# A two-block transformer kernel: other order of the attention heads in block 2, and its query copies issued by ScalarE

## The chip, the cores and the metric

The kernel runs on one core of a Trainium2 chip. Its time is the device time of one execution in microseconds. Engines are named as in the profile: PE is TensorE (PEld its weight loads), DVE is VectorE, ACT is ScalarE, POOL is GpSimd, SP is SyncE. A name with a q (SPq, ACTq) is the engine's sequencer, which also issues DMAs.

## The reference

Input x is 512 tokens by 1024. Block 1 (once) mixes latent attention and a state-space scan. Block 2 runs twice, layer 0 and layer 1; the change lies in its attention. Cut to what matters:

```python
def second_block(x, ...):
    for l in range(2):
        h = rms_norm(x, g_pre_mix[l])
        nq, kc, vc, ksel, vsel, kwin, vwin, gates, fq, fk, fv, ff = split(h @ w_in[l])
        o_nsa = nsa_mixer(nq, kc, vc, ksel, vsel, kwin, vwin, gates, ...)   # 8 heads of 64, 2 kv groups
        o_fox = fox_mixer(fq, fk, fv, ff, b_forget[l])                      # 8 heads of 64
        x = x + rms_norm(concat([o_nsa, o_fox]) @ w_out[l], g_post_mix[l])
        h = rms_norm(x, g_pre_mlp[l])
        x = x + rms_norm(square(relu(h @ w_up[l])) @ w_down[l], g_post_mlp[l])

# nsa, per head: a gated sum of three attentions of one query: over 31 compressed keys
#   (a small MLP over blocks of 32 tokens), over selected blocks, over a window; the last
#   two use rotary queries and keys, and with 512 tokens both see every earlier key.
# fox, per head: causal attention with logits q.k/8 + cum[i] - cum[j], cum = cumsum(log_sigmoid(f))
```

All of it is float32.

## The kernel before

**Arithmetic.** A float32 number is held as a high and a low part (ACT casts the high part, L143; DVE or POOL subtracts for the low part, L144 and L864), and one product is three matmuls (L174 to L176). A projection job is 24 such matmuls of 512 columns, and its weights (512 KB) come by one DMA on SP's queue (L153), then a high cast on ACT and a low part on DVE.

**Heads in pairs.** Queries and keys are worked on two heads at a time, 64 rows each: four nsa pairs n0 to n3 and four fox pairs f0 to f3 in each layer. An nsa pair is four runs of `attend` (two heads by two branches) and a fox pair is two. One `attend` makes scores on PE (L914 with the high, L917 with the low query), masks and takes the minimum on DVE (L918), exponentials on ACT (L921), scales on POOL (L930), transposes on PE (L943), splits (L143 and L144), and makes the values on PE (L952, L953).

**The doubled query.** A score matmul has the high and low parts of the keys stacked in its 128 rows, so the 64 rows of a query must stand there twice. `doubled` (L869) casts each head's high half (L874, L875), subtracts the low half on POOL (L864), and copies all four to the other 64 rows by DMAs of 128 KB, one `move` (L866) each: two called qh, two called ql. Eight pairs in two layers make 16 doublings and 64 moves, 32 qh and 32 ql. In the kernel before, SP issues them (L867), in one queue with all weight loads.

**What sets the order.** The program is written as generators that interleave: `rounds` runs the heads in the order of the list ORDER, and between the pieces of a head `fill` and `chunk` put pieces of the projections, in the order of the list PROJ; (0, m) is the nsa query of pair m, (1, m) the fox query, (2, m) the fox key. A scheduler with a simulated timeline then orders the instructions of each engine. Every engine and every queue works in order, so an instruction that waits holds what stands behind it. Successive projections use one PSUM bank: the next starts once ACT has copied the last out (`raw`, L1109).

**The start of a layer.** After two matmul groups for the keys (`kf`, L1083), projections run until raw (0, 0) is there, so n0's query and, by the scheduler, one more stand ahead of the compress matmuls `cps` (L983), which need weights that SP loads (L980, x9 at a time). Rotary copies of nsa queries go by small DMAs that ACT issues (`swap`, L1068). The list ORDER also sets the layout in which the pairs are summed by the output weights w_out_t, whose loads and matmuls for the finished pairs (`early`) run beside the last heads.

Of the kernel before, what the change touches and what calls it, by code (L numbers as in the profile page):

```python
# [9 lines left out]
F32 = mybir.dt.float32  # L10
# [9 lines left out]
EPS = 1e-6  # L20
NEG = -1e30
SLOTS1 = {"S": 6, "PT": 4, "E": 2, "et": 1, "K": 1, "T": 3, "Y": 1, "sq": 3, "c": 2, "PW": 1, "U": 1, "C": 1, "w": 4}
PROJ = ((0, 0), (2, 0), (1, 0), (0, 1), (2, 1), (1, 1), (0, 2), (2, 2), (1, 2), (0, 3), (2, 3), (1, 3))
ORDER = "n0 f0 n1 f1 n2 f2 n3 f3".split()
PRE = 10
R0, C0, LEAD, RATE0, RATE, AHEAD = 0, 1, 1, 1.3, 0.4, 5
HEAD0 = (0, 3, 6, 9)
# [36 lines left out]
class Net:  # L64
# [799 lines left out]
        self.nc.gpsimd.tensor_tensor(out, src, hi.bitcast(F32), OP.subtract)  # L864

    def move(self, out, src):  # L866
        self.nc.sync.dma_start(out.bitcast(F32), src.bitcast(F32))  # L867

    def doubled(self, src, tag):  # L869

# [127 lines left out]
    def layer(self, l, normed, x_dram, out=None):  # L998
# [86 lines left out]
        foxt, nsat, cht, raw = {}, {}, {}, {}  # L1085

        jobs = [("k" if i == 2 else "q", i, m) for i, m in PROJ]
        loaded = []
# [6 lines left out]
        def project(j):  # L1095

            _, i, m = jobs[j]
            if j == 0:
                load()
            wh, wl = loaded[j]  # L1100
            p = self.ps("mm")
            for k in range(8):
                if k == AHEAD:
                    load()
                self.mm3(self.tiled(p), wh[k], wl[k], xh[k], xl[k], k == 0, k == 7)
                if k < 7:
                    yield
            r = raw[i, m] = self.act(name="raw", tag="S")
            nc.scalar.activation(r, p, AF.Copy, scale=-0.125 if i == 2 else 1.0)  # L1109
            if i == 0:  # L1110
                yield
                nsat[m] = self.doubled(rope(r, None), "Q")
            elif i == 1:
                foxt["q", m] = self.doubled(r, "Q")
            else:
                foxt["k", m] = self.stacked(r, "PT")

        def ensure(i, m):
            while m not in nsat if i == 0 else ("qk"[i - 1], m) not in foxt:
                self.chunk()  # L1120
            yield

        self.fillers, self.pe = [project(j) for j in range(len(jobs))], None
        while (0, 0) not in raw:
            self.chunk()
        kk = []
        for kf in kfs:
            rope(kf, kf)
            kk.append(self.stacked(kf, "K"))
        for _ in ensure(0, 0):  # L1130
            pass

        def bank(d, tag):

# [120 lines left out]
        def early():  # L1255
# [8 lines left out]
            for n in range(2 * EB):  # L1264
                while (ORDER[n][0], int(ORDER[n][1])) not in whole:
                    yield
                self.mm3(p, *(x[:, 0:128] for x in mixed[ORDER[n][0], int(ORDER[n][1])]), wo[0][n], wo[1][n], n == 0, False)
                part.append(n)
# [18 lines left out]
        r = R0  # L1287
        for pair in ORDER:
            m = int(pair[1])
# [21 lines left out]
        xT, xh, xl = self.new_xT()  # L1311
        mixed = [mixed[p[0], int(p[1])] for p in ORDER]
        for half in range(2):
# [139 lines left out]
def layout(i):  # L1453
# [11 lines left out]
    w = n("w_out_2").reshape(L, 2, 4, 128, 2, 512)  # L1465
    w = np.stack([w[:, "nf".index(p[0]), int(p[1])] for p in ORDER], axis=1)
    A["w_out_t"] = w.reshape(L, 4, 2, 128, 2, 512).transpose(0, 4, 1, 3, 2, 5)
# [59 lines left out]
```

## Time and profile before

| what | us |
| --- | --- |
| time, median of 3 runs | 1667.33 (1665.48 to 1668.69) |
| the profiled execution | 1673.57 |
| its span, first to last instruction | 1671.8 |
| attention of layer 0, from its first kf to the MLP's transposes | 391.4 to 639.8 |
| attention of layer 1, the same | 1051.8 to 1313.9 |
| PE busy in the span | 1593.8 (95%) |
| ACT busy in the span | 794.3 (48%) |

The profiled execution took 6.24 us more than the median of the runs, and 1.77 us of it lie around the span. Busy shares are averages: in a stage where PE is nearly always busy, the few places where it is idle say which other engine or transfer is late there. Beside busy time, the granted clock says at which speed PE worked.

### The profile page before, as it was taken

To read this page: it belongs to the slowest core of one execution; us is meant where nothing else is said; L and a number is where in the kernel's file an instruction comes from. 1 tells how busy PE (TensorE), PEld (TensorE's weight loads), DVE (VectorE), ACT (ScalarE), POOL (GpSimd) and SP (SyncE) were. 2 spreads that over 40 slices of the span, in tenths; PEclk is the share of its full clock that TensorE was granted. 3 is DMA by queue.
4 is the path that set the end of the run, shared out by engine and by line. 5 is a ranking of instruction groups with operands and counts; after the bars stand their busy time and mean duration, and the time that the engine had idled before them with its cause. 6 is when DMAs were issued, how large, how long until landed. Compare 5 with 4: busy or idle time off the path is not lost.

```text
span 1671.8 us, 22665 instructions
## 1 busy us (share of the span) xinstructions
PE 1593.8 (95%) x8240; PEld 1345.8 (80%) x8240; DVE 951.2 (57%) x1863; ACT 794.3 (48%) x1548; POOL 402.4 (24%) x492
## 2 busy tenths in 40 slices
PE   7996899999999999999999999999989999999998
PEld 6884687787888888888888888788868888888886
DVE  8978767754687865323333365478875532333334
ACT  6634476543677845333232444368774433323242
POOL 2000013313455712001010140345580210101012
PEclk9998899999999999999999999899999999999999
DMA  5211452544322442332333334512234133333332
GB/s 172 75 56 38 129 146 76 184 119 156 92 59 53 119 134 75 96 95 89 101 101 101 114 109 128 161 45 58 64 102 126 51 101 101 101 101 101 101 96 81
DMA packets 71407, 167.44 MB, mean 100 GB/s; under 512 B 14464, under 2 KB 23168, under 8 KB 71296
## 3 DMA queue, kind: packets, MB, share of 16 engines
q1 hardware_dynamic: 70528, 165.21, 32.3%
q8 instruction: 65, 1.06, 0.3%
q10 hardware_dynamic: 768, 0.79, 0.2%
q14 instruction: 46, 0.38, 0.1%
HBM read 145.80 MB, written 10.98 MB: 94 GB/s over the span
## 4 chain that ended last, share of the span: by engine, by line
PE 70%; DVE 7%; ACT 3%; issue 3%; DMA 2%; POOL 1%; ACTq 1%; DVEq 0%; POOLq 0%; SPq 0%
PE mm L176 19%; PE mm L174 19%; PE mm L175 19%; PE cps L983 2%; PE ptr L943 2%; DVE sc L918 1%; DVE pt L144 1%; PE sc L917 1%; PE sc L914 1%; PE oacc L952 1%; PE oacc L953 1%; DVE wlo L144 1%; ACT ysq L206 1%; DMA ql<-ql 1%; ACT sc L921 1%
## 5 line engine op out<-in xcount | busy, mean ns | idle before, releaser
L144 DVE TENSOR_TENSOR wlo<-wst,whi 128x1024 fp32r<-128x1024 f32 (+3 forms) x209 | 253.7, 1218 | 248.8 <-ACT whi L143 245.1
L174 PE MATMUL mm<-xT,whi 128*128 128x512 f32 (+1 forms) x896 | 337.8, 380 | 4.3 <-ACT kf L1083 2.8
L143 ACT CAST whi<-wst 128x1024 fp32r<-128x1024 f32 (+3 forms) x209 | 215.3, 1034 | 256.6 <-PE mm L176 123.7
L175 PE MATMUL mm<-xT,whi 128*128 128x512 f32 (+1 forms) x896 | 335.5, 376 | 0.0
L176 PE MATMUL mm<-xT,wlo 128*128 128x512 f32 (+1 forms) x896 | 326.3, 376 | 0.9 <-DVE wlo L144 0.8
L1367 POOL TENSOR_TENSOR relu<-relu 128x512 f32<-128x512 f32 x64 | 67.1, 1048 | 539.6 <-ACT relu L1366 539.6
L176 PE MATMUL mm<-whi,hl 128*128 128x512 f32 x512 | 195.9, 389 | 0.0
L175 PE MATMUL mm<-wlo,hh 128*128 128x512 f32 x512 | 195.9, 389 | 0.0
L174 PEld LDWEIGHTS mm<-xT,whi 128*128 128x128 f32 x896 | 168.2, 189 | 33.4 <-ACT kf L1083 3.6
L176 PEld LDWEIGHTS mm<-xT,wlo 128*128 128x128 f32 x896 | 168.7, 189 | 32.1 <-DVE wlo L144 1.8
L175 PEld LDWEIGHTS mm<-xT,whi 128*128 128x128 f32 x896 | 168.9, 189 | 27.4
L174 PE MATMUL mm<-whi,hh 128*128 128x512 f32 x512 | 188.2, 389 | 0.0
L921 ACT ACTIVATE sc<-sc,mn 128x512 f32<-128x512 f32 x192 | 107.1, 559 | 32.9 <-DVE mn L918 25.2
L144 DVE TENSOR_TENSOR hl<-relu,hh 128x512 fp32r<-128x512 f32 x64 | 51.8, 810 | 119.4 <-ACT hh L143 117.1
L144 DVE TENSOR_TENSOR pt<-ptr,pt 128x256 fp32r<-128x256 f32 (+1 forms) x160 | 95.7, 605 | 40.0 <-ACT pt L143 39.1
L176 PEld LDWEIGHTS mm<-whi,hl 128*128 128x128 f32 x512 | 96.1, 188 | 20.0
L175 PEld LDWEIGHTS mm<-wlo,hh 128*128 128x128 f32 x512 | 96.1, 188 | 19.9
L174 PEld LDWEIGHTS mm<-whi,hh 128*128 128x128 f32 x512 | 96.1, 188 | 19.9
L1366 ACT ACTIVATE relu<-mm 128x512 f32<-128x512 f32 x64 | 38.3, 598 | 148.3 <-PE mm L176 148.3
L918 DVE CUSTOM_DVE_ANT_0 sc<-sc,c_mask 128x512 f32<-128x512 f32 x192 | 87.3, 483 | 34.2 <-PE sc L917 30.9
L143 ACT CAST pt<-ptr 128x256 fp32r<-128x256 f32 (+1 forms) x160 | 81.5, 515 | 52.4 <-PE ptr L943 41.3
L930 POOL TENSOR_SCALAR sc<-sc,smx,gt 128x512 f32<-128x512 f32 (+3 forms) x128 | 78.9, 627 | 82.9 <-DVE smx L925 54.4
(394 smaller groups left out, 2961.5 us busy)
## 6 DMA issues: line engine op xcount, KB each, us to landing
wst<-in_w_up_t SPq DMA_DIRECT2D x64, 512.0 KB
wst<-in_w_down_t SPq DMA_DIRECT2D x64, 512.0 KB
wst<-in_w_in_m SPq DMA_DIRECT2D x24, 512.0 KB
wst<-in_w_in_a SPq DMA_DIRECT2D x16, 512.0 KB
x<-x SPq DMA_DIRECT2D x32, 256.0 KB
w<-in_cw SPq DMA_DIRECT2D x32, 256.0 KB
wst<-in_w_out_t SPq DMA_DIRECT2D x16, 512.0 KB
wst<-in_w_in SPq DMA_DIRECT2D x8, 512.0 KB
```

The source lines that it names most:

```text
L143: self.nc.scalar.copy(hi, src)
L144: self.nc.vector.tensor_tensor(lo, src, hi.bitcast(F32), OP.subtract)
L174: mm(ps, lh, rh, start=first, stop=False)
L175: mm(ps, lh, rl, start=False, stop=False)
L176: mm(ps, ll, rh, start=False, stop=last)
L918: nc.vector.tensor_tensor_reduce(out=sreg[i], in0=p, in1=self.mask[:, 512 - w:512], scale=1.0, scalar=3e38, op0=OP.add, op1=OP.min, accum_ ...
L921: self.mark = nc.scalar.activation(sreg[i], sreg[i], AF.Exp, bias=mn[:, i:i + 1], scale=-1.0, accum_out=sm[:, i:i + 1])
L930: nc.gpsimd.tensor_scalar(sreg[i], sreg[i], sm[:, i:i + 1], rgate[:, i:i + 1], OP.mult, OP.mult)
L943: self.pe = nc.tensor.transpose(p[:, c:c + 128], sreg[i][:, j * 128:(j + 1) * 128], self.ident)
L983: nc.tensor.matmul(p[:, :62], st[:, j], bk[:, jj].rearrange("p g n -> p (g n)"), start=jj == 0, stop=jj == 15)
L1366: nc.scalar.activation(a, p, AF.Relu)
L1367: nc.gpsimd.tensor_tensor(a, a, a, OP.mult)
```

## The change

The order of the pairs becomes f0 n0 f1 n1 f2 n2 f3 n3 instead of n0 f0 n1 f1 n2 f2 n3 f3. The projections of pair m come as fox key, fox query, nsa query. At the start of a layer, projections run until f0's query is doubled instead of until n0's is projected, and n0's doubling is no longer finished ahead of the heads. All `move` DMAs are issued by ACT instead of SP.

```diff
-PROJ = ((0, 0), (2, 0), (1, 0), (0, 1), (2, 1), (1, 1), (0, 2), (2, 2), (1, 2), (0, 3), (2, 3), (1, 3))
-ORDER = "n0 f0 n1 f1 n2 f2 n3 f3".split()
+PROJ = tuple((i, m) for m in range(4) for i in (2, 1, 0))
+ORDER = "f0 n0 f1 n1 f2 n2 f3 n3".split()
...
     def move(self, out, src):
-        self.nc.sync.dma_start(out.bitcast(F32), src.bitcast(F32))
+        self.nc.scalar.dma_start(out.bitcast(F32), src.bitcast(F32))
...
-        while (0, 0) not in raw:
+        while ("q", 0) not in foxt:
             self.chunk()
...
-        for _ in ensure(0, 0):
-            pass
```

ACT at the start of layer 0, before. A row is line, operation, out<-in; whi is the high cast of a projection's weights, kf and raw copy PSUM out (raw_3800 is the first projection), swap the rotary DMA, ka and kb the stacked keys:

```order
L1083 ACTIVATE kf_3761<-mm_3736 128x512
L143 CAST whi_3912<-wst_3910 128x1024
L1068 DMA swap1_3285<-kf_3761 8x512 x4
L143 CAST whi_4040<-wst_4038 128x1024
L1109 ACTIVATE raw_3800<-mm_3769 128x512
L889 CAST ka_3810<-kf_3734 64x512
L890 CAST kb_3811<-kf_3734 64x512
L1068 DMA swap0_3284<-raw_3800 8x512 x2
L889 CAST ka_3824<-kf_3761 64x512
L890 CAST kb_3825<-kf_3761 64x512
L1068 DMA swap0_3284<-raw_3800 8x512 x2
L1109 ACTIVATE raw_3938<-mm_3862 128x512
```

The same place of the changed kernel, whose first cast (whi_3826) now stands between the swap DMAs of the first kf and the copy of the second:

```order
L1068 DMA swap0_3284<-kf_3734 8x512
L143 CAST whi_3826<-wst_3824 128x1024
L1068 DMA swap0_3284<-kf_3734 8x512 x3
L1083 ACTIVATE kf_3761<-mm_3736 128x512
L1068 DMA swap1_3285<-kf_3761 8x512 x4
L143 CAST whi_3943<-wst_3941 128x1024
L143 CAST whi_4099<-wst_4097 128x1024
L1109 ACTIVATE raw_3800<-mm_3769 128x512
L889 CAST ka_3802<-raw_3800 64x512
L890 CAST kb_3803<-raw_3800 64x512
L1109 ACTIVATE raw_3839<-mm_3808 128x512
L874 CAST qh1_3841<-raw_3839 64x512
```

Ahead of raw_3800 now stands the cast whi_4099 of the fifth weight block, which takes the buffer of the first projection's weights and so waits for its last matmul. A third projection (mm_3893, copied out as raw_3969) comes before the compress matmuls, which on PE begin behind two before.

The same stretch on PE before (mm are projections, cps the compress matmuls):

```order
L174 MATMUL mm_3862<-xT_2959,whi_3787 128x512
L175 MATMUL mm_3862<-xT_2961,whi_3787 128x512
L176 MATMUL mm_3862<-xT_2959,wlo_3788 128x512
L983 MATMUL cps_3855<-bk_3638,w1_3856 128x62 x4
L983 MATMUL cps_3855<-bk_3638,w1_3866 128x62 x4
```

and in the changed kernel, where mm_3893 is the third projection:

```order
L174 MATMUL mm_3893<-xT_2959,whi_3826 128x512
L175 MATMUL mm_3893<-xT_2961,whi_3826 128x512
L176 MATMUL mm_3893<-xT_2959,wlo_3827 128x512
L983 MATMUL cps_3886<-bk_3638,w1_3887 128x62 x4
L983 MATMUL cps_3886<-bk_3638,w1_3897 128x62 x4
```

The cps are the same, 24 matmuls of a projection later.

SP's queue near the end of layer 1's attention, before (wst are weights of the output, qh and ql the moves of f3, the last pair):

```order
L153 DMA wst_11756<-in_w_out_t 128x1024
L153 DMA wst_11764<-in_w_out_t 128x1024
L153 DMA wst_12165<-in_w_out_t 128x1024
L867 DMA qh1_11683<-qh1_11683 64x512
L867 DMA qh2_11684<-qh2_11684 64x512
L191 DMA gain_12439<-in_g_post_mlp 128x512
L191 DMA gain_12440<-in_g_post_mlp 128x512
L867 DMA ql1_11685<-ql1_11685 64x512
L867 DMA ql2_11686<-ql2_11686 64x512
L153 DMA wst_12171<-in_w_out_t 128x1024
```

ACT of the changed kernel at f3 of layer 0 (raw_5527 is f3's query; sc are exponentials of earlier heads, pt casts of their transposes):

```order
L1109 ACTIVATE raw_5527<-mm_5362 128x512
L143 CAST pt_5380<-ptr_5398 128x256
L874 CAST qh1_5529<-raw_5527 64x512
L875 CAST qh2_5530<-raw_5527 64x512
L921 ACTIVATE sc_5579,smx_5583<-sc_5579,mn_5582 128x512
L921 ACTIVATE sc_5580,smx_5583<-sc_5580,mn_5582 128x384
L143 CAST pt_5456<-ptr_5459 128x512
L143 CAST whi_5473<-wst_5471 128x1024
L867 DMA qh1_5529<-qh1_5529 64x512
L867 DMA qh2_5530<-qh2_5530 64x512
L867 DMA ql1_5531<-ql1_5531 64x512
L143 CAST mix_5452<-oacc_5521 64x512
```

The moves left SP's queue, where they stood behind weight and gain loads, and stand in ACT's, where here four instructions (the two exponentials, a cast pt and a weight cast) come between the casts of the query and the DMAs that copy it.

## Rows read from the trace of the kernel before

**Rows 1.** The page: busy time by engine

```profile
PE 1593.8 (95%) x8240; PEld 1345.8 (80%) x8240; DVE 951.2 (57%) x1863; ACT 794.3 (48%) x1548; POOL 402.4 (24%) x492
```

**Rows 2.** Windows of both attention stages: length, busy by engine, PE clock, DMA

```profile
391.40:639.80 248.40, 237.54 (x1366) 203.14 (x1364) 180.90 (x485) 162.77 (x398) 124.32 (x159) 1.00 0.33 99
1051.80:1313.90 262.10, 245.36 (x1366) 210.57 (x1364) 181.82 (x485) 161.98 (x398) 122.23 (x157) 0.96 0.31 90
```

**Rows 3.** Timeline of PE, layer 0: start, us, [idle before <-releaser]

```profile
395.99 0.50 PE L174 MATMUL mm<-xT,whi 128*128 128x512 f32 x1 [1.70 <-ACT kf L1083]
402.43 0.50 PE L174 MATMUL mm<-xT,whi 128*128 128x512 f32 x1 [0.69 <-ACT raw L1109]
...
408.01 7.25 PE L983 MATMUL cps<-bk,w 128*128 128x62 f32 x64
...
581.02 0.65 PE L917 MATMUL sc<-ka,ql 128*128 128x512 f32 x2 [0.24 <-DMA ql<-ql]
```

**Rows 4.** Timeline of PE, layer 1

```profile
1055.72 0.50 PE L174 MATMUL mm<-xT,whi 128*128 128x512 f32 x1 [1.06 <-ACT kf L1083]
1062.23 0.50 PE L174 MATMUL mm<-xT,whi 128*128 128x512 f32 x1 [0.76 <-ACT raw L1109]
...
1070.52 11.66 PE L983 MATMUL cps<-bk,w 128*128 128x62 f32 x56 [1.70 <-DMA w<-in_cw]
...
1198.19 0.47 PE L914 MATMUL sc<-ka,qh 128*128 128x512 f32 x1 [1.05 <-DMA qh<-qh]
...
1243.87 0.47 PE L914 MATMUL sc<-ka,qh 128*128 128x512 f32 x1 [2.32 <-DMA qh<-qh]
...
1248.11 1.19 PE L917 MATMUL sc<-ka,ql 128*128 128x512 f32 x3 [1.61 <-DMA ql<-ql]
```

**Rows 5.** Windows of 5 us in layer 1: granted clock third from the end

```profile
1070.00:1075.00 5.00, 4.48 (x24) 4.48 (x24) 0.69 (x1) 1.83 (x3) 2.48 (x3) 0.62 0.58 192
1075.00:1080.00 5.00, 5.00 (x25) 5.00 (x25) 1.58 (x2) 1.54 (x3) 3.65 (x3) 0.50 0.29 62
1080.00:1085.00 5.00, 5.00 (x20) 4.42 (x20) 1.31 (x5) 1.90 (x3) 0.00 (x1) 0.52 0.80 231
...
1245.00:1250.00 5.00, 3.02 (x12) 2.32 (x11) 2.79 (x8) 1.37 (x7) 3.64 (x6) 0.52 0.59 149
1250.00:1255.00 5.00, 5.00 (x21) 4.09 (x20) 1.09 (x9) 1.83 (x7) 2.85 (x5) 0.79 0.00 0
```

**Rows 6.** Chain of waits, layer 1: start, us, what

```profile
1063.83 6.65 DMA w<-in_cw
...
1239.00 0.63 ACT qh L875
...
1241.61 6.37 DMA ql<-ql
```

**Rows 7.** Chain of waits, layer 0, a move

```profile
576.98 3.90 DMA ql<-ql
```

**Rows 8.** Issues by line: duration in ns, min/median/max

```profile
L867 SPq DMA_DIRECT2D qh<-qh x32: 462/467/567, 415.6 to 1239.8; - x32
L1068 ACTq DMA_DIRECT2D swap<-raw x32: 631/632/661, 402.6 to 1207.8; - x32
```

**Rows 9.** Timeline of ACT in layer 0: casts, copies, exponentials

```profile
538.21 0.60 ACT L1109 ACTIVATE raw<-mm 128x512 f32<-128x512 f32 x1 [2.34 <-PE mm L176]
538.71 0.37 ACT L143 CAST pt<-ptr 128x256 fp32r<-128x256 f32 x1
...
539.54 0.58 ACT L143 CAST pt<-ptr 128x512 fp32r<-128x512 f32 x1 [0.47 <-PE ptr L943]
...
540.02 1.05 ACT L143 CAST whi<-wst 128x1024 fp32r<-128x1024 f32 x1
...
541.66 0.72 ACT L921 ACTIVATE sc<-sc,mn 128x512 f32<-128x512 f32 x1 [0.59 <-DVE cs L1225]
...
542.39 0.60 ACT L921 ACTIVATE sc<-sc,mn 128x384 f32<-128x384 f32 x1
```

## The prediction

> **What bounds the kernel now.** The page comes first: PE is busy for 1593.8 of 1671.8 us [rows 1], so time can only come from PE's few idle places and from its clock. The change touches only the attention of block 2, so the windows of its two stages come next. They do the same work, 1366 matmul groups each, and layer 1 takes 262.1 us where layer 0 takes 248.4: 13.7 more. PE's mean clock is 0.96 there against 1.00 [rows 2]. What layer 1 loses and layer 0 does not is what a change of order could win; the timeline of PE names the places [rows 3, 4].
>
> At the start of layer 1 PE waits 1.06 for the key copy, 0.76 between two projections and 1.70 for the compress weights, and the granted clock then falls from its upper level to 0.50, the lower one (1.2 GHz of 2.4), for most of 15 us [rows 4, 5]. Layer 0 waits 1.70 and 0.69 at the first two places, not at all for the compress weights, and keeps its clock [rows 2, 3]. Near the end of layer 1, PE waits 1.05 for a qh move, then for f3, the last pair, 2.32 for qh and 1.61 for ql, and the clock falls again [rows 4, 5]. The chain of waits shows why: the query's second cast ends at 1239.63, the ql move is issued at 1241.61 and is 6.37 us under way [rows 6], where a like move in layer 0 took 3.90 [rows 7].
>
> **The change part by part, against the profiled execution (1673.57).**
>
> *Start of layer 1.* The compress weights land at 1063.83 + 6.65 = 1070.48 [rows 6], 1.70 after PE asked. One more projection now stands ahead of the compress matmuls. In layer 0 one took from 402.43 to 408.01, 5.58 us [rows 3]. That covers the 1.70 and leaves 3.9 for what is late next, the one more weight block of 512 KB ahead of them on SP. So the stall goes (bounds: 0 to 1.70 left): -1.70. The clock loss is busy time times the missing share: 4.48 x 0.38 + 5.00 x 0.50 + 5.00 x 0.48 = 6.6 [rows 5]. As a check, 56 compress matmuls took 11.66 here, and 64 took 7.25 in layer 0 [rows 3, 4]: at that rate 6.3, so 5.3 was lost in these alone. I count the 6.6 as gone, because the stall just ahead of the fall goes; the rivals price the opposite.
>
> The same start gets new costs, in both layers. A weight cast (1.05 [rows 9]) stands ahead of the copy of the first projection and waits for the same last matmul: PE's wait there grows by 1.05. The third projection adds one more such boundary, 0.69 to 0.76 [rows 3, 4]. A cast also stands ahead of the second key copy: 0 if the rotary DMAs around it take longer anyway, 1.05 at most; I take 0.7. Sum 2.5 a layer (bounds 1.7 to 2.9). Layer 1's start: -1.70 - 6.6 + 2.5 = -5.8. Layer 0's start: +2.5.
>
> *End of layer 1.* The last pair is now n3, four runs of attention, where f3 was two. f3 comes earlier and its moves no longer stand behind output weights and gains. Its waits, 2.32 + 1.61, go, and so does the 1.05 at 1198 [rows 4]. The fall that follows cost 3.02 x 0.48 + 5.00 x 0.21 = 2.5 [rows 5]. Sum -7.5 (bounds: 0, if a nearly same wait returns elsewhere, to -7.5). The output matmuls that fill the end need whole pairs, and seven of eight are whole before the last pair as they were: nothing counted.
>
> *f3 of layer 0.* This is the place where the new order looks worse. Four instructions now separate the query's casts from its DMAs on ACT: 0.72 + 0.60 + 0.58 + 1.05 = 2.95 [rows 9], and the last of them, a weight cast, waits for a DMA of its own. In the kernel before, f2 in a like place waited only 0.24 for its move [rows 3], that is, it had nothing to spare. So up to 0.24 + 2.95 = 3.2 is late, and 0 if the fillers stretch; I take 3.0, near the end that the order points to.
>
> *ACT issues the moves.* 64 issues leave SP, which has room, and enter ACT's queue, which also makes the exponentials and the casts that PE waits for. On SP one takes 0.467; on ACT a smaller rotary DMA took 0.632 [rows 8]: 64 x 0.467 = 30 to 64 x 0.632 = 40 us of ACT's sequencer, on top of 162.77 + 161.98 busy in 248.4 + 262.1 [rows 2]. Beside that, the ql moves wait on ACT for POOL's subtraction, and whatever exponential stands behind waits with them. ACT has a third of the stage free, and an issue can run beside the execution of the instruction ahead: at 538.84 to 541 rotary DMAs were issued beside two casts, and the next exponential waited 0.59 [rows 9]. Bounds for the path: 0 and +40. I take a tenth of 30, +3.0: as in the 0.59, only a part of each burst shows, and PE usually has filler matmuls that do not depend on ACT.
>
> Sum: -5.8 + 2.5 - 7.5 + 3.0 + 3.0 = -4.8, so 1668.8 for a profiled execution. The profiled one stands 6.24 above the median of 1667.33; at the same ratio (1667.33 / 1673.57) that is 1662.5.
>
> **A rule against the change.** Row first: the late ql move was under way 6.37 with weights loading beside it, and the other 3.90 [rows 6, 7]. The Trainium skill, DMA: Bandwidth & Descriptors, section "Issuing engines are not separate DMA queues", says that DMAs of all issuing engines run on the same 16 DMA engines and interleave, and that issuing from several saves only sequencer time. By it the moves would land no sooner from ACT, and the DMA half of the change would have only its cost. The section on queues, rings and completion order of the same page gives SP and ACT a row of rings each, served in turn, by which a move on ACT's row would overtake queued weights. No row before shows a move issued by ACT. My sum counts nothing for a faster landing, so it stands by either; if the second holds, up to 6.37 - 3.90 = 2.5 at a late move is to be had more.
>
> **The rivals.**
>
> *ACT's queue becomes the bound (slower).* One mechanism: 64 issues and the waits for POOL hold ACT in order, exponentials and casts come late, and PE runs out of fillers within each attention. For: ACT is busy two thirds of these stages. Against: PE's listed waits there are mostly for DMAs, not for ACT. At a third of 40 on the path this is +13 instead of +3, and a late f3 that also drops the clock costs another 2.5: -4.8 + 10.3 + 2.5 = +8, so 1681.6 profiled, 1675 measured. It decides once each move costs PE more than (4.8 + 3.0) / 64 = 0.12 us.
>
> *The clock falls at the layer starts all the same (no change).* The waits at the start of layer 1 would be 1.76, 1.81 and 0.76, together 4.3, in place of 1.06 + 0.76 + 1.70 = 3.5 that preceded the fall; layer 0's 2.4 would become 4.9. For: more idle time than before. Against: it is spread over one more projection, and the single stall of 1.70 just ahead is gone. If one layer loses 6.6, the time is -4.8 + 6.6 = +1.8: 1669.1 measured; both, +8.4, 1675.7.
>
> *A larger gain.* Moves land early, f3 of layer 0 is covered by fillers, and issues run beside execution: both costs of 3.0 are nil and 2.5 more is saved on waits: -13.3, 1654. For: layer 1 would then about reach what layer 0 shows today. Against: f3's order on ACT.
>
> **How the numbers follow.** Forecast 0.37, ACT's queue 0.22, one fall of the clock 0.17, both 0.08, larger gain 0.16. A measurement of this kernel tells 0.2%, 3.3 us, from no change. Faster (below 1664.0) is most of the forecast's own spread (0.33) and the larger gain: 0.49. Slower (above 1670.7) is ACT's queue, both falls and a little of one: 0.32. The same: 0.19. The forecast's own range is 1658 to 1667; the one that holds 8 of 10 reaches into the larger gain and to the slower cases: 1653 to 1676.
>
> **What would show it.** Right: in layer 1 no wait of PE for in_cw, and a clock of 1.00 at the compress matmuls; no waits of 2.32 and 1.61 near the end; waits of about 1.8 at the copy of the first projection in both layers; a wait of some 3 us for qh of f3 in layer 0; ACT's idle time ahead of exponentials little changed. Wrong: stage lengths of 248 and 262 that grow by several us each with waits for ACT's exponentials and casts spread through them, or a granted clock near 0.5 after either layer's start.

## The result and the profile after

The changed kernel is slower: 1686.7 us median of 4 runs (1682.39 to 1690.12) against 1666.4 of the kernel before, a ratio of 1.012 (95% interval 1.0098 to 1.0142), some 20 us. The forecast was 1662.5, 4.8 below the median of 1667.33 that it started from.

The page and the windows of the two attention stages, after (busy time by engine, then PE's clock, DMA share, GB/s):

```profile
PE 1603.6 (95%) x8240; PEld 1348.6 (80%) x8240; DVE 948.0 (56%) x1863; ACT 793.3 (47%) x1548; POOL 405.3 (24%) x492
```

```profile
392.90:655.40 262.50, 245.82 (x1365) 207.42 (x1363) 177.84 (x485) 161.46 (x398) 126.33 (x159) 0.97 0.31 93
1068.90:1325.40 256.50, 241.27 (x1366) 204.70 (x1364) 181.90 (x485) 161.54 (x398) 123.31 (x157) 0.99 0.32 92
```

Layer 1 became 5.6 shorter than in [rows 2], as forecast in sign, though a second execution of the kernel before will take this back. But layer 0, which had nothing wrong with it, became 14.1 longer, and its clock, 1.00 before, is 0.97. The timeline of PE, after, at the places of [rows 3, 4]:

```profile
397.68 0.50 PE L174 MATMUL mm<-xT,whi 128*128 128x512 f32 x1 [1.87 <-ACT kf L1083]
404.83 0.50 PE L174 MATMUL mm<-xT,whi 128*128 128x512 f32 x1 [1.41 <-ACT raw L1109]
411.25 0.50 PE L174 MATMUL mm<-xT,whi 128*128 128x512 f32 x1 [0.69 <-ACT raw L1109]
...
449.79 1.08 PE L1207 MATMUL c3ps<-w2v,hv 128*128 128x64 f32 x8 [0.86 <-DVE hv L1200]
...
575.65 0.66 PE L943 MATMUL ptr<-c_ident,sc 128*128 128x128 f32 x2 [2.56 <-DVE smx L925]
584.83 0.73 PE L914 MATMUL sc<-kb,qh 128*128 128x512 f32 x3 [0.50 <-DMA qh<-qh]
...
1246.57 0.38 PE L914 MATMUL sc<-kb,qh 128*128 128x256 f32 x1 [1.34 <-DVE mn L918]
1249.30 0.41 PE L943 MATMUL ptr<-c_ident,sc 128*128 128x128 f32 x2 [1.87 <-DVE smx L925]
```

The three waits at the start of layer 0 are those of the working: the key copy, the copy behind the cast, the added boundary. The wait of 2.56 is new. Windows of 5 us around it (granted clock third from the end) show what follows, as [rows 5] did for layer 1:

```profile
570.00:575.00 5.00, 2.94 (x18) 2.10 (x16) 4.38 (x16) 5.00 (x16) 3.57 (x4) 0.96 0.21 83
575.00:580.00 5.00, 4.35 (x17) 4.09 (x18) 4.90 (x15) 3.62 (x10) 4.15 (x7) 0.50 0.48 162
580.00:585.00 5.00, 4.50 (x19) 3.39 (x18) 1.29 (x3) 0.37 (x1) 2.69 (x3) 0.86 0.73 230
```

PE is busy for 2.94 of 5 us and then runs at 0.50. Why VectorE is late there stands in the chain of waits, after, from 568 us on (start, us, what):

```profile
568.69 3.50 DMA swap<-raw
...
572.31 0.91 DVE swap L1069
...
574.04 0.86 DVE r L1071
...
575.50 0.08 DVE smx L925
...
575.65 1.09 PE ptr L943 x4
...
578.59 6.20 DMA qh<-qh
```

This is n3's query, in the new order the last of all projections. Being an nsa query it needs the rotary step: a swap DMA (3.50), then two operations on VectorE, whose queue holds the softmax of the heads running just then. After the step come the casts and moves, the first 6.20 us under way, and PE waits again at 584.83. In the kernel before, the last projection was f3's query, which needs no rotary step.

### The profile page after: what moved, and what is told of

Same layout as the page of the kernel before. It is cut to its first block, busy times and chain, and to the rows that moved or that the text cites. A ratio compares the mean times of both kernels' runs of the same rounds, so it can differ in the third digit from the quotient of the medians.

```text
span 1684.8 us, 22628 instructions
## 1 busy us (share of the span) xinstructions
PE 1603.6 (95%) x8240; PEld 1348.6 (80%) x8240; DVE 948.0 (56%) x1863; ACT 793.3 (47%) x1548; POOL 405.3 (24%) x492
## 4 chain that ended last, share of the span: by engine, by line
PE 57%; DVE 4%; ACT 2%; DMA 1%; POOL 1%; issue 1%; ACTq 0%; DVEq 0%; POOLq 0%
PE mm L174 17%; PE mm L175 17%; PE mm L176 17%; PE ptr L943 2%; DVE sc L918 1%; ACT ysq L206 1%; PE oacc L953 1%; PE oacc L952 1%; PE cps L983 1%; PE sc L914 1%; PE sc L917 1%; DVE pt L144 1%; POOL rs_r L201 0%; PE xtr L221 0%; POOL rs_t L199 0%
```

## The experiments

All times are medians, but for `before_again` and `after_again`, which are single executions. The ratio is to the runs of the kernel before on the same chip. The labels ran on several chips, where the kernel before took 1665.2 to 1667.1, so a difference between two labels carries a few us of noise.

| label | heads | first of the last pair's projections | moves | us | ratio, 95% interval |
| --- | --- | --- | --- | --- | --- |
| (before) | old | n3's query | SP | 1665 to 1667 | 1 |
| moves_on_act | old | n3's query | ACT | 1666.84 | 1.0003 (0.9976 to 1.003) |
| order_only | new | f3's key | SP | 1686.89 | 1.0141 (1.011 to 1.0173) |
| (changed) | new | f3's key | ACT | 1686.7 | 1.012 (1.0098 to 1.0142) |
| end_only_q_first | last pair new | n3's query | ACT | 1672.37 | 1.0026 (1.0002 to 1.005) |
| new_end | last pair new | f3's key | ACT | 1682.11 | 1.0094 (1.0061 to 1.0127) |
| n3_query_first | new | n3's query | ACT | 1678.08 | 1.0073 (1.0052 to 1.0094) |

**Halves of the change, and both kernels again.** `order_only` is the changed kernel with one line back, `moves_on_act` the kernel before with that line alone:

```diff
-        self.nc.sync.dma_start(out.bitcast(F32), src.bitcast(F32))
+        self.nc.scalar.dma_start(out.bitcast(F32), src.bitcast(F32))
```

> New order of pairs and projections, moves back on SP. Theory A (ACT's in-order queue is the loss: 64 issues and their waits): the loss of 20 us goes, 1660 to 1668. Theory B (the new order is the loss: two more boundaries between projections at each layer start and waits inside layer 0): most of it stays, 1680 to 1688. Theory C (each half costs about half): about 1676.

> Old order, moves issued by ACT. Theory A: 1680 to 1687, with waits of PE for the chain of minima, exponentials and transposes grown in both layers. Theory B: within 3 us of the kernel before, 1664 to 1670. Theory C: about 1676.

The issues on ACT cost nothing that can be measured (the interval is -4 to +5 us), and the new order alone gives the whole loss. Theory A, ACT's queue, falls. The 64 issues are on ACT and as long as bounded; here of `moves_on_act` (ns: min, median, max):

```profile
L867 ACTq DMA_DIRECT2D qh<-qh x32: 468/523/1200, 413.4 to 1230.4; - x32
L867 ACTq DMA_DIRECT2D ql<-ql x32: 467/468/609, 414.8 to 1233.5; - x32
```

They run beside the execution of ACT's other work, and even ahead of it. On the timeline of ACT, after, the two qh moves of f3 in layer 0 are issued as the second cast of the query ends, while three of the four instructions that stand ahead of them in ACT's order (the second exponential, the cast pt and the weight cast) begin only later:

```profile
552.96 0.62 ACT L875 CAST qh<-raw 64x512 fp32r<-64x512 f32 x1
553.60 0.72 ACT L921 ACTIVATE sc<-sc,mn 128x512 f32<-128x512 f32 x1
553.62 1.12 ACTq L867 DMA_DIRECT2D qh<-qh  x2
...
555.39 1.05 ACT L143 CAST whi<-wst 128x1024 fp32r<-128x1024 f32 x1
```

The stages of `moves_on_act` are 250.80 and 244.90 us, against 249.20 and 252.90 with SP in `before_again`; its profiled execution, 1659.07, was the fastest of its ten.

> The kernel before, unchanged, a second profile of it. If the waits of PE of 1.70 for in_cw and of 2.32 and 1.61 for the last moves and the falls of the clock in layer 1 belong to the kernel, its attention stage of layer 1 is again about 262 us against 248 of layer 0; if they were particular to one execution, layer 1 is several us shorter and the time nearer to 1666.

1665.06. Its attention stages:

```profile
389.80:639.00 249.20, 237.50 (x1366) 203.20 (x1364) 181.23 (x485) 162.92 (x398) 123.78 (x159) 1.00 0.33 98
1052.40:1305.30 252.90, 239.19 (x1366) 204.56 (x1364) 183.03 (x486) 162.02 (x398) 122.53 (x157) 0.99 0.31 94
```

Layer 1 took 252.9, not 262.1. The wait of 1.70 for in_cw and the fall of the clock at the compress matmuls [rows 4, 5] are not there. The windows over the compress matmuls, which begin at 1068.45 here:

```profile
1067.00:1072.00 5.00, 5.00 (x40) 4.70 (x38) 0.00 (x0) 1.98 (x4) 4.19 (x4) 1.00 0.93 316
1072.00:1077.00 5.00, 5.00 (x41) 4.64 (x39) 2.26 (x2) 1.84 (x4) 3.37 (x3) 1.00 0.33 113
```

The late moves of f3 are there, here again of the kernel before on the timeline of PE:

```profile
1235.62 0.47 PE L914 MATMUL sc<-ka,qh 128*128 128x512 f32 x1 [2.32 <-DMA qh<-qh]
...
1239.33 1.19 PE L917 MATMUL sc<-ka,ql 128*128 128x512 f32 x3 [1.12 <-DMA ql<-ql]
```

So 8.3 of the forecast's gain belonged to one execution of two, and against this one the changed kernel's layer 1 (256.5) is 3.6 longer.

> The changed kernel, unchanged, a second profile of it. If its two falls of the clock in the attention of layer 0 (about 6 us) belong to the kernel they come again at the same places, near 450 and near 575 us, and the stage is again about 262 us; if not, the stage is near 256 and falls lie elsewhere.

1687.63, stages of 262.5 and 256.9, clock below 1.00 between 449 and 459, at 574 to 579 and at 584 to 589; the wait of 2.56 is there again, and the one for n3's qh is 2.05 instead of 0.50. These belong to the changed kernel.

**Where in the order.** `old_start` is n0 f0 f1 n1 f2 n2 f3 n3 with the layer's start as before, and `new_end` exchanges only f3 and n3 and projects n3's query last, as the changed kernel does. `n3_query_first` and `compress_later` change one line of the changed kernel (the comments name the run):

```diff
-PROJ = tuple((i, m) for m in range(4) for i in (2, 1, 0))
+PROJ = tuple((i, m) for m in range(4) for i in ((2, 1, 0) if m < 3 else (0, 2, 1)))   # n3_query_first
...
-PRE = 10
+PRE = 4                                                                               # compress_later
```

> Moves on ACT. Order n0 f0 f1 n1 f2 n2 f3 n3: the first pair as before, the other three as in the changed kernel. Theory S (the loss of the order is made at the start of the layers: one more boundary, a later compress step and the fall of the clock near 450): back near the kernel before, 1662 to 1672. Theory E (it is made where the last nsa query comes late, f3 and n3): stays at 1680 to 1688. Theory P (every pair pays some): 1677 to 1683.

> Moves on ACT. Order n0 f0 n1 f1 n2 f2 f3 n3: only the last pair exchanged. Theory S: as before, 1664 to 1670. Theory E: most of the loss, 1677 to 1688. Theory P: about 1671.

> The changed kernel, but in the last pair the nsa query is projected ahead of the fox key and query. In the changed kernel PE waits 2.56 us near 575 in layer 0 and 1.87 near 1249 in layer 1 for VectorE, which has the rotary step of that query in its queue, and the clock falls behind both. Theory E: those waits and falls go, some 8 us less, 1677 to 1681. Theory S: they make place for like ones elsewhere, 1683 to 1690.

> The changed kernel with PRE = 4 instead of 10, so that only two of the eight compress groups of four stand ahead of the heads and f0's scores begin earlier. Theory S: the stalls near 450 (0.60 and 0.86) and the fall of the clock behind them change with it, by 3 us a layer or more in either direction; if the fall goes, 1679 to 1683. Theory E: no change, 1684 to 1689.

`old_start` 1689.21 (just above its highest range) and `compress_later` 1686.44: neither the start of the layers nor the place of the compress step, by itself, gives the time back. `new_end` 1682.11: one exchanged pair at the end, its nsa query last, makes most of the loss. `n3_query_first` 1678.08: 8.6 come back by projecting the same query earlier (its copy stands 141.4 us into layer 0 instead of 173.0). The stretch from the copy of the last projection to the last value matmul shows it. First the changed kernel, then `n3_query_first`, both layers (length, PE busy first):

```profile
565.90:625.00 59.10, 54.37 (x297) 44.84 (x296) 39.69 (x112) 35.13 (x88) 23.48 (x33) 0.94 0.40 126
1238.70:1295.20 56.50, 51.59 (x290) 42.85 (x290) 43.48 (x115) 34.12 (x87) 24.21 (x34) 0.97 0.41 123
```

```profile
559.40:615.70 56.30, 53.02 (x305) 44.21 (x305) 39.37 (x124) 37.35 (x95) 26.12 (x38) 1.00 0.42 131
1228.80:1284.70 55.90, 52.60 (x306) 44.16 (x306) 38.72 (x120) 37.59 (x95) 26.08 (x37) 1.00 0.41 123
```

PE's idle time in it (length less busy) falls from 4.7 and 4.9 to 3.3 and 3.3, and the clock goes from 0.94 and 0.97 to 1.00. By busy time times the missing share, an estimate, the clock is worth 54.4 x 0.06 + 51.6 x 0.03 = 4.8, and with 3.0 of idle time that is 7.8, near the 8.6. In `moves_on_act`, where two runs of attention are left behind the last projection and not four, the same stretch is short and has 0.2 and 1.2 in the profiled execution:

```profile
573.40:608.30 34.90, 34.70 (x202) 29.97 (x201) 24.62 (x71) 22.46 (x57) 16.26 (x23) 1.00 0.64 197
1228.50:1265.80 37.30, 36.11 (x204) 30.71 (x203) 24.80 (x70) 22.27 (x58) 16.42 (x24) 1.00 0.59 182
```

**The end alone.** The only edit to `moves_on_act` in `end_only_q_first`, where n3's query stays ahead of f3's projections:

```diff
-ORDER = "n0 f0 n1 f1 n2 f2 n3 f3".split()
+ORDER = "n0 f0 n1 f1 n2 f2 f3 n3".split()
```

`old_start_q_first` is `old_start` with n3's query first; `spread_fillers` and `act_spread` set RATE2 to 0.4 instead of 0.6, in `n3_query_first` and in `moves_on_act`.

> Moves on ACT, all projections in the old order, only the last two pairs exchanged in the list: n0 f0 n1 f1 n2 f2 f3 n3, so n3's query is projected ahead of f3's. Theory E1 (the loss at the end is the late rotary step of n3's query): within 4 us of the kernel before, 1664 to 1670. Theory E2 (it is that four runs of attention instead of two are left behind the last projection, with too few other matmuls to fill): 1672 to 1680, with more idle time of PE from the last projection to the last value matmul than the 0.2 and 1.2 us of the old order with moves on ACT.

> Moves on ACT. Order n0 f0 f1 n1 f2 n2 f3 n3, with n3's query projected first in the last pair. Beside the kernel with the changed order and n3's query first (1678), it takes back the start of the layers: 1.6 to 1.9 us less idle time of PE at the start of each layer. If that start is a loss of its own: 1673 to 1676. If the exchange only shifts where the idle time lies: 1677 to 1683.

> The changed kernel with n3's query projected first, and the output matmuls that fill between the last heads doled out at a rate of 0.4 instead of 0.6. Theory E2: spreading them over the longer end helps, 1672 to 1677. If the fillers there wait for whole pairs anyway and not for the rate: 1676 to 1681.

> Old order, moves on ACT, output matmuls doled out at 0.4 instead of 0.6: an attempt at a version faster than both kernels. With the old order PE is idle for 0.2 and 1.2 us from the last projection to the last value matmul, so there is little to win: 1662 to 1669.

`end_only_q_first` 1672.37: with the query early, the exchange at the end costs about 5 (0.3 to 8 by its interval), so most of `new_end` is the late query and a smaller part the longer end. Its last stretch has 4.8 and 3.9 us of idle time:

```profile
564.00:620.50 56.50, 51.66 (x290) 41.79 (x289) 37.21 (x116) 36.76 (x93) 24.65 (x37) 1.00 0.39 131
1225.80:1281.80 56.00, 52.07 (x289) 43.67 (x288) 37.68 (x116) 36.17 (x93) 24.63 (x36) 0.97 0.40 123
```

With `new_end` and the two kernels of the new order this makes a square: late instead of early costs 1682.1 - 1672.4 = 9.7 with the other pairs old, and 1686.7 - 1678.1 = 8.6 with them new. The first is rough: the six runs of `new_end` are three at 1677.9 to 1678.6 and three at 1685.6 to 1687.8. Counted from the kernel before on each one's own chip, the two differences are 11.6 and 7.5. `old_start_q_first` 1687.84 missed both its ranges: it has the short waits at the layer start (0.69 instead of 1.41) and others between the pairs instead, so the start can't be read from it. `spread_fillers` 1682.14 (4 above `n3_query_first`) and `act_spread` 1671.65 (1.0026, 1.0 to 1.0052) lie above all their ranges: a lower rate isn't what the end lacks, and no version run here beats the kernel before.

**What the late query costs, and what is left.** In `q_first_123` pairs 1 to 3 have their nsa query first; in `no_rope_late` and `no_rope_first` the rotary step of n3 is left out:

```diff
-                nsat[m] = self.doubled(rope(r, None), "Q")
+                nsat[m] = self.doubled(r if m == 3 else rope(r, None), "Q")
```

> The changed kernel, with the nsa query projected first in pairs 1, 2 and 3 (the projections as before but for the first pair). If the late nsa queries of the middle pairs cost as n3's does: 1668 to 1674, the level of the old order with only the end exchanged (1672). If what is left over is the layer start: 1676 to 1681, as with n3's query alone put first (1678).

> The changed kernel without the rotary step of n3's query (left out of the computation in both layers: four small DMAs, two VectorE and one POOL instruction each). If the late rotary step is what the late query costs: about 9 us less than the changed kernel, 1675 to 1680, and no wait of PE near 575 in layer 0. If the late projection costs by something else (its moves, its place among the heads): 1683 to 1688.

> The same left out, with n3's query projected first: the control. If the rotary step matters only when it is late, nearly the time with it, 1675 to 1680, and so within 3 us of no_rope_late; if the late query costs by something else, still 7 to 10 us below no_rope_late.

Without the rotary step the late query costs 1678.96 - 1674.05 = 4.9 instead of 8.6, so it seems a part of the cost, not all; the difference of 3.7 goes across chips. The wait of 2.56 near 575 is gone, as expected. But `no_rope_first` is 4.9 below `no_rope_late` and not within 3 of it. The timeline of PE of `no_rope_late`, layer 0, shows what is left there, waits for the moves of the same late query:

```profile
568.68 0.47 PE L914 MATMUL sc<-kb,qh 128*128 128x512 f32 x1 [1.25 <-DMA qh<-qh]
571.40 0.64 PE L917 MATMUL sc<-kb,ql 128*128 128x512 f32 x2 [1.10 <-DMA ql<-ql]
```

In layer 1 the trace has a wait of 2.07 ahead of the matmul with n3's ql, put down to POOL. The attention over compressed keys, which also starts from the late query, was not tested apart.

`q_first_123` came out at 1697.2, 10 above the changed kernel and outside both ranges. Now the fox queries of pairs that begin with fox are the late ones; on the timeline of PE, in layer 1:

```profile
1249.12 0.76 PE L914 MATMUL sc<-ka,qh 128*128 128x512 f32 x1 [3.86 <-DMA qh<-qh]
```

It does not tell the start from the middle. That whichever query is projected last before its heads is paid for would fit this row, but is not shown: in layer 0 the longest wait is another, 3.51 for VectorE, and in `n3_query_first`, where f3's query is last too, no wait for its moves is over 0.5.

## Why the prediction was wrong

*Start of layer 1, -5.8.* After, there is no wait for in_cw and no fall of the clock at the compress matmuls, as said. But `before_again` shows neither in the kernel before. The 1.70 and 6.6 were of one execution; the profiled execution stood 6.24 above the median, and the prediction scaled that away instead of asking which of its waits made it.

*Start of each layer, +2.5.* Right in kind, and too high by a third (its lower bound was 1.7): PE's idle time from the key copy to the third projection's copy is 3.97 in layer 0 after and 2.40 up to the third copy of `before_again`, and 3.80 against 2.13 in layer 1: +1.6 and +1.7.

*End of layer 1, -7.5. This is the step that failed.* It said that f3's waits go and that n3 at the end costs nothing. f3's waits went, and waits for VectorE with n3's rotary step in its queue came, 1.34 and 1.87: idle time in the last stretch of layer 1 is no better than in `before_again` (56.5 - 51.6 = 4.9 against 44.2 - 39.2 = 5.0), and only the clock is (0.97 against 0.92). The same stretch of `before_again`, both layers:

```profile
571.10:606.70 35.60, 34.88 (x201) 29.75 (x200) 24.20 (x69) 22.32 (x57) 16.20 (x24) 1.00 0.60 190
1229.50:1273.70 44.20, 39.24 (x205) 32.31 (x204) 23.43 (x70) 23.61 (x57) 16.53 (x24) 0.92 0.49 153
```

And the step was priced only where the old order had a wait. Layer 0 had none, and there the same new end cost 4.7 of idle time against 0.7 before and a clock of 0.94. In place of -7.5, the new end alone (`new_end`) measured 1682.1 against 1665.2, +16.9 over both layers. What was missed is that the last query is now an nsa one, with the rotary step and the moves behind it, and four runs of attention after it. The order of PROJ, in the diff, said so; the working followed f3's moves and did not follow n3's. Nor had SP's queue been what held f3's moves. On the timeline of SP's sequencer, before:

```profile
1239.19 1.10 SPq L867 DMA_DIRECT2D qh<-qh  x2
...
1241.61 1.81 SPq L867 DMA_DIRECT2D ql<-ql  x2
```

The casts ended at 1238.97 and 1239.63, and POOL's first subtraction, by the chain of waits, at 1241.59: each pair of moves was issued within 0.3 us of its data, and the 6.37 came after.

*f3 of layer 0, +3.0.* Not seen: PE has no wait for f3's qh there. The working let the moves wait for four instructions to execute; the rows of ACT above have both issued from 553.62 on, and the second cast ended at 553.58. The wait of 2.56 is of another cause and the move that PE waits for at 584.83 is n3's.

*ACT issues the moves, +3.0, and the rival with 30 to 40 us.* The ratio of 1.0003 (0.9976 to 1.003) rules out the 30 to 40 and the rival's 13; it does not tell 3.0 from nothing. The rival's time, 1675, and that of both falls of the clock, 1675.7, were the nearest, 11 short, the first for a wrong reason. By the rule cited from the Trainium skill (DMA: Bandwidth & Descriptors, "Issuing engines are not separate DMA queues") a change of the issuer saves only the sequencer's time; `moves_on_act` against the kernel before agrees in time. n3's move was 6.20 us under way on ACT's queue; one such row does not settle whether a move lands sooner from there.

*The rival on the clock* had falls at the wrong place: layer starts kept 1.00 in the changed kernel, with 1.87, 1.41 and 0.69 of idle time in 14 us; the falls came near 450 and 575. It was not far off, though: in `n3_query_first`, with the same three waits in layer 0, the clock did fall behind the first:

```profile
394.00:399.00 5.00, 5.00 (x15) 3.97 (x16) 0.77 (x2) 1.04 (x1) 0.00 (x0) 0.66 0.65 224
```

What stays open: of the 20 us, the late query is about 9 (7.5 to 11.6) and the exchanged end about 5; the other 5 or so, from the new start and the middle pairs, were not taken apart. The added waits at the layer starts, 1.6 + 1.7, would be most of it, but both runs that were to show it have new waits elsewhere. The fall near 450 is a second candidate, and it has a like one in layer 1. Windows of the changed kernel:

```profile
450.00:455.00 5.00, 4.52 (x22) 3.35 (x22) 3.04 (x9) 2.42 (x7) 0.99 (x2) 0.67 0.15 36
455.00:460.00 5.00, 5.00 (x24) 4.57 (x24) 1.38 (x2) 1.81 (x3) 0.00 (x0) 0.65 0.00 0
...
1124.00:1129.00 5.00, 3.55 (x19) 2.91 (x20) 3.46 (x14) 2.34 (x9) 2.49 (x5) 0.85 0.00 0
1129.00:1134.00 5.00, 5.00 (x30) 4.17 (x28) 2.75 (x5) 2.75 (x5) 0.00 (x0) 0.80 0.00 0
```

By busy time times the missing share, an estimate, they cost 3.2 and 1.5. In all nine traces of kernels with the new start of a layer the clock falls to 0.50 at this place, 55 to 60 us into the stage, in both layers; in none of the eight with the old start does it fall there. So this belongs to the new start, and the prediction priced only its waits. But `old_start`, which has neither these falls nor the added waits, was no faster (1689.21), so what they cost in the end is not shown. No run separates the fall near 450 from the waits of 0.60 and 0.86 ahead of it.

## What to carry to other kernels

When an order of work is turned round, ask what is now made last and how long its chain is from there to its first use: the last item has little other work left to hide behind, and here a query with a rotary step in that place cost about 9 us, and 4.9 with the step left out. Price a moved step in every repetition of the stage, also where nothing was wrong before. And where a profiled execution stands well above the median, take a wait from it as the kernel's own only if a second execution shows it too.

## What the runs showed of the hardware

DMA issues on ACT, 32 of a median 523 ns and 32 of 468, stood between exponentials and casts in ACT's order without a measurable cost (ratio 1.0003, 0.9976 to 1.003). The sequencer issued two of them at 553.62 although a weight cast that stood ahead of them in that order began only at 555.39. A wait of PE of some 2.5 us with 2.94 of 5 us busy was followed by a granted clock of 0.50 to 0.86 for the next 10, so by an estimate the fall cost 4.35 x 0.50 + 4.50 x 0.14 = 2.8, about as much as the wait.
